# Reordering the first loads and casts of a two-layer hybrid decoder trunk

## The chip, the cores and the metric

The kernel runs on one core of one Trainium2 chip. The metric is the device time of one execution in microseconds (us). The kernel before took 1221.57 us, the median of 3 runs (1221.18 to 1221.61). The profiled execution, from which all the rows below come, took 1221.98 us.

## The reference, cut to what matters

The input `x` is 512 tokens by 1024 features, in float32. Two layers follow each other. Each has a token mixer and a gated ConvFFN, and each of the four sublayers ends in `LayerNorm(alpha * x + f(x))`. The mixer of layer 0 is gated linear attention (GLA), the mixer of layer 1 gated DeltaNet. Only the very beginning of GLA is touched by the change:

```python
def gla_mixer(x, w_in, w_gk2, b_gk, norm_w, w_out):
    hk, hv = GLA_HEADS * GLA_DK, GLA_HEADS * GLA_DV          # 512, 1024
    proj = x @ w_in                                          # w_in: 1024 x 3088
    q, k, v, gate, gk_lr = jnp.split(proj, [hk, 2 * hk, 2 * hk + hv, 2 * hk + 2 * hv], axis=-1)
    gk = jax.nn.log_sigmoid((gk_lr @ w_gk2 + b_gk).astype(jnp.float32)) / GLA_NORMALIZER
    ...
```

## The kernel before, in words

**Products.** Every float32 operand is split into two fp32r parts, `h` (a cast) and `l` (what the cast loses): `xh`, `xl` for x, `wh`, `wl` for a weight. A product is then three matmuls, `wh*xh + wh*xl + wl*xh`. The cast is normally made by ScalarE (ACT) and the subtraction by VectorE (DVE); `split_out` (L715) records both. TensorE (PE) is the engine with the most work.

**x.** x is loaded in eight tiles of 128 tokens by 512 features, called `h` (names h_99 and so on, 256 KB each). The two tiles that hold tokens 0 to 127 and 128 to 255 of features 0 to 511 are h_99 and h_101, here called the first quarters. The other halves of the same tokens are h_100 and h_102, and the later tokens are h_103 to h_106. `x_part` (L766) turns a tile with four PE transposes into a bank `xT` and splits it into `xh` and `xl`.

**Weights of the projection.** An item `fm` is a block of 128 columns of `w_in`, 1024 by 128, loaded into a buffer `raw` (512 KB; three such buffers). The first two items (raw_109 and raw_114) are loaded, cast and used in two halves of 256 KB. The third item is `rep`, a small one (64 KB), the fourth is raw_219, loaded whole. `open_items` (L522) multiplies the first two items with the first 256 tokens, half by half. The `rep` item and raw_219 follow, on the first 256 tokens and then on the rest.

**v's weights.** v and the gate are made by a scheme with seven products of quarter size. Some of its weight quarters, named `b11`, are kept in buffers `gw` (two of 512 KB) over several products, and loaded by `gated_load` (L438) as far ahead as the plan looks. The first products of this scheme come after all items of q and k.

**What sets the order.** The kernel is written in program order, and a scheduling layer places each instruction on its engine. `keep_in_program_order` pins an instruction. `behind(a, b)` (L703) says that `a` stands after `b` in the order, and adds no wait by itself. Each engine then runs its own instructions strictly in this order and waits on semaphores. DMA transfers are issued by SyncE (SP, most of them), by ACT (`nc.scalar.dma_start`) and by GpSimd (POOL). Transfers issued by SP go into one hardware queue (q1), those of ACT into another (q10), those of POOL into a software queue (q0). All of them run on the same 16 DMA engines.

**The opening.** `load_x` (L776) issues the two first quarters, then `prefetch`, which issues the first weights. It records a copy on ACT that loads an activation table, and three products `warm` of a column of ones, which need nothing but a memset. These keep PE busy from the start of the kernel on. Then come the cast of the first half weight (`split(0)`), the two `x_part`s, and `behind` calls that fix how ACT and DVE interleave these.

Of the kernel before, what the change touches and what calls it, by code (L numbers as in the profile page):

```python
# [17 lines left out]
S = 512  # L18
NTB = S // P
NC = D // P  # L20
# [14 lines left out]
GATED_NEW = {"b21": "b21", "b11": "b11", "t1": "b12", "b22": "b22"}  # L35
# [37 lines left out]
def blk(i, n=P):  # L73
    return slice(i * n, i * n + n)


class Trunk:
# [214 lines left out]
    def issue(self, item):  # L292

        nc = self.nc
        if item[0] == "rep":
            return self.issue_rep(*item[1:])
        if item[0] == "pad":
            return self.issue_pad(*item[1:])
        if item[0] == "fold":
            return self.issue_fold(*item[1:])  # L300
        if item[0] == "gated":
            return self.issue_gated(*item[1:])
        raw = self.rp.tile([P, 1024], F32, name=self.uid("raw"), tag="raw")
        used = 1024
        if item[0] == "fm":
            _, w, col = item
            r3 = raw.rearrange("p (c f) -> p c f", c=NC)
            w3 = w[:, col:col + P].rearrange("(c p) f -> p c f", p=P)
            part = lambda queue, c, n: queue.dma_start(r3[:, c:c + n, :], w3[:, c:c + n, :])
            if self.issued > 1:  # L310
                part(nc.sync, 0, NC)
            else:
                if self.issued == 0:
                    part(nc.scalar, 0, 4)
                    self.arriving(0, 1)
                else:
                    part(nc.sync, 0, 4)
                    self.arriving(1, 1)
                self.late.append(lambda: part(nc.sync, 4, 4))
                if self.issued:  # L320
                    for load in self.late:
                        load()
        else:
            _, w, row, n, col, _ = item
            used = n * S
            self.load = nc.sync.dma_start(
                raw[:, :used].rearrange("p (j f) -> p j f", j=n),
                w[row:row + n * P, col:col + S].rearrange("(j p) f -> p j f", p=P))
        if self.in_slots(item):
            w = []  # L330
            for j in range(used // S):
                wh, wl = self.room("wsh"), self.room("wsl")
                self.slotted = self.split_out(wh, wl, raw[:, blk(j, S)])
                self.vec(0.7)
                w.append((wh, wl))
            return w
        self.held += 1
        wh = self.wp.tile([P, 1024], F32R, name=self.uid("wh"), tag="wh")
        wl = self.wp.tile([P, 1024], F32R, name=self.uid("wl"), tag="wl")
        pieces = [blk(j, S) for j in range(used // S)] if self.issued < 2 else [slice(0, used)]  # L340
        split = lambda cols: self.split_out(wh[:, cols], wl[:, cols], raw[:, cols])
        if self.issued < 2:
            self.pieces += [lambda cols=cols: split(cols) for cols in pieces]
        elif self.issued < 4:
            self.opening(*split(pieces[0]))
        else:
            self.split = parts = split(pieces[0])
            for ins, other in zip(parts, self.after):
                if other is not None:
                    self.behind(ins, other)  # L350
        self.vec(1.24)
        return [(wh[:, blk(j, S)], wl[:, blk(j, S)]) for j in range(used // S)]
# [85 lines left out]
    def gated_load(self, group, name, i):  # L438


        if name not in GATED_NEW:
            return
        if name == "b11":
            t = self.mp.tile([P, 1024], F32, name=self.uid("gw"), tag="gw", bufs=2)
        else:
            t = self.rp.tile([P, 1024], F32, name=self.uid("raw"), tag="raw")
        self.nc.sync.dma_start(t.rearrange("p (j f) -> p j f", j=2), self.gated_rows(group, GATED_NEW[name], i))
        group[name, i] = t

    def issue_gated(self, group, name, i):  # L450
# [325 lines left out]
    def load_x(self, x):  # L776

        nc = self.nc
        self.h = [[self.resid("h") for _ in range(2)] for _ in range(NTB)]

        def load(tb, hf):
            nc.sync.dma_start(self.h[tb][hf], x[blk(tb), blk(hf, S)])
            self.set(("h", tb, hf))


        for tb in range(2):
            load(tb, 0)
        self.arriving = load
        self.look = 2
        self.prefetch()  # L790
        self.look = 0

        self.tc.keep_in_program_order(nc.scalar.copy(self.warm, self.one))
        ps = self.psum("warm")
        ones = self.one.to_broadcast([P, S])
        for n in (S, S, 64):
            self.tc.keep_in_program_order(
                nc.tensor.matmul(ps[:, :n], ones[:, :P], ones[:, :n], start=True, stop=True))
        split = lambda i: self.pieces[i]()
        piece = split(0)  # L800
        first = self.x_part(0, 0)
        second = self.x_part(1, 0)

        self.behind(first[0], piece[0])
        self.behind(second[0], first[0])
        self.behind(second[1], first[1])
        self.behind(piece[1], second[1])
        self.first = (second[0], piece[1])
        self.opening(*split(2))

        def arrive(i):
            self.opening(*self.x_part(i, 1))
            self.opening(*split(2 * i + 1))
            if i:
                self.look = 1
                self.prefetch()
                for tb in range(2, NTB):
                    for hf in range(2):
                        load(tb, hf)
                self.look = LOOKAHEAD  # L820
                self.prefetch()

        self.arrive = arrive
        for tb in range(2):
            self.set(("x", tb))

        def second():
            for tb in range(2, NTB):
                for hf in range(2):
                    self.last = self.x_part(tb, hf)  # L830
                yield 1.2

        self.spawn(second(), 7.0)
# [1235 lines left out]
```

## Time and profile before

| What | us |
|---|---|
| median of the runs | 1221.57 |
| the profiled execution's own time | 1221.98 |
| its span, from the first to the last instruction | 1220.2 |
| PE busy in it | 1213.6 |
| DVE busy | 906.1 |
| ACT busy | 609.4 |
| GpSimd busy | 160.7 |

The span is 1.78 us shorter than the execution's own time: this much lies around it. The profiled execution took 0.41 us longer than the median of the runs. All times in rows of the trace are microseconds from the start of the span. A row of the timeline gives start, duration, engine, line, operation, `output<-input`, shape and number of instructions, and in brackets the time for which the engine was idle before it and what ended that. `SPq` and `ACTq` are the issuing parts of these engines, `PEld` is PE's loading of weights, which overlaps its products. PE rows of products overlap each other, because products are pipelined: the time that one takes from the stream is the distance from its start to the next start. A row of the DMA issues ends with the time from the issue to the landing.

### The profile page before, as it was taken

The page shows a single profiled execution, that of the slowest core. Times are in us where ns is not written, and L with a number is a line of the kernel's source. Part 1 is how long each engine was busy: PE and PEld are TensorE (multiplying, and loading weights), DVE is VectorE, ACT ScalarE, POOL GpSimd, SP SyncE. Part 2 cuts the span into 40 slices and gives each one's busy share as a digit, 9 for nine tenths or more (in the row PEclk, how much of TensorE's full clock was granted, in tenths as well). Part 3 has the DMA queues.
Part 4 walks back from the last instruction along what each step waited for, and adds up shares of the span by engine and source line. Part 5 has one row for each costly group of instructions (what it writes and reads, how often), then busy time and mean ns, then how long its engine had stood idle before and what let it go on. Part 6 is the DMA issues. An engine that isn't in the chain of part 4 may idle for free.

```text
span 1220.2 us, 17190 instructions
## 1 busy us (share of the span) xinstructions
PE 1213.6 (99%) x6501; PEld 1025.1 (84%) x6501; DVE 906.1 (74%) x1515; ACT 609.4 (50%) x1072; POOL 160.7 (13%) x203
## 2 busy tenths in 40 slices
PE   9999999999999999999999999999999999999998
PEld 8888888988888888889888888988988888888886
DVE  6989787787757675666789965688687757776667
ACT  5666663544434443454678555544644433443440
POOL 3030101601100110001242030200510100020000
PEclk9999999999999999999999999999999999999999
DMA  8384642536743554433444351335444853383311
GB/s 227 113 164 115 141 154 72 189 105 137 190 122 92 124 95 121 123 102 91 125 125 130 87 136 36 101 107 156 135 125 101 170 178 95 104 171 97 108 65 69
DMA packets 176275, 149.41 MB, mean 122 GB/s; under 512 B 16870, under 2 KB 140842, under 8 KB 176192
## 3 DMA queue, kind: packets, MB, share of 16 engines
q1 hardware_dynamic: 162464, 116.28, 32.2%
q0 software_dynamic: 12768, 31.37, 13.0%
q8 instruction: 51, 0.84, 0.3%
q10 hardware_dynamic: 960, 0.66, 0.2%
q14 instruction: 32, 0.26, 0.1%
HBM read 129.92 MB, written 5.78 MB: 111 GB/s over the span
## 4 chain that ended last, share of the span: by engine, by line
PE 97%; DMA 1%; ACT 1%; DVE 1%; SPq 0%; issue 0%; DVEq 0%
PE fm L213 54%; PE fold L213 19%; PE tm L213 15%; PE o L213 2%; PE xT L231 1%; DMA raw<-in_gla_w_in_dram 1%; PE pq L213 1%; PE pg L213 1%; PE vn L213 1%; PE yT L231 1%; PE V L213 0%; PE ds L213 0%; PE qs L213 0%; PE s L213 0%; PE ks L213 0%; DMA raw<-in_gdn_w_in_dram 0%
## 5 line engine op out<-in xcount | busy, mean ns | idle before, releaser
L213 PE MATMUL fm<-xh,wh 128*128 128x512 f32 (+2 forms) x1096 | 400.4, 368 | 0.7 <-ACT xh L716 0.7
L213 PE MATMUL fm<-xl,wh 128*128 128x512 f32 (+2 forms) x1096 | 398.5, 366 | 0.0
L213 PE MATMUL fm<-xh,wl 128*128 128x512 f32 (+1 forms) x1072 | 391.5, 367 | 0.2 <-DVE wl L716 0.2
L716 DVE TENSOR_TENSOR wl<-raw,wh 128x1024 fp32r<-128x1024 f32 (+1 forms) x158 | 195.4, 1239 | 151.7 <-ACT wh L716 151.3
L716 ACT CAST wh<-raw 128x1024 fp32r<-128x1024 f32 (+1 forms) x159 | 164.9, 1039 | 211.2 <-PE fm L213 135.5
L213 PEld LDWEIGHTS fm<-xh,wh 128*128 128x128 f32 (+1 forms) x1096 | 205.4, 188 | 34.1 <-ACT xh L716 0.9
L213 PEld LDWEIGHTS fm<-xl,wh 128*128 128x128 f32 (+1 forms) x1096 | 205.4, 188 | 32.6
L213 PEld LDWEIGHTS fm<-xh,wl 128*128 128x128 f32 x1072 | 201.2, 189 | 33.7 <-DVE wl L716 0.4
L1019 DVE SCALAR_TENSOR_TENSOR conv<-fm,ffn_cw,conv 128x511 f32<-128x511 f32 x112 | 83.5, 745 | 9.6 <-ACT conv L1017 7.9
L213 PE MATMUL fold<-wh,fh 128*128 128x512 f32 x224 | 87.6, 391 | 0.0
L213 PE MATMUL fold<-wh,fl 128*128 128x512 f32 x224 | 87.2, 389 | 0.0
L213 PE MATMUL fold<-wl,fh 128*128 128x512 f32 x224 | 87.1, 389 | 0.0
L716 ACT CAST wh<-b 128x1024 fp32r<-128x1024 f32 x48 | 50.0, 1054 | 74.2 <-PE fold L213 32.5
L716 DVE TENSOR_TENSOR wl<-b,wh 128x1024 fp32r<-128x1024 f32 x48 | 58.1, 1222 | 22.7 <-ACT wh L716 22.5
L412 POOL DMA_DIRECT2D b<-b x24 | 20.8, 902 | 357.2 <-DVE wl L716 306.7
L1037 ACT ACTIVATE conv<-conv 128x512 f32<-128x512 f32 x44 | 27.8, 632 | 63.3 <-DVE conv L1019 63.3
L1585 DVE SCALAR_TENSOR_TENSOR conv<-fm,gdn_cw,conv 128x511 f32<-128x511 f32 (+2 forms) x72 | 54.0, 788 | 5.1 <-ACT conv L1583 4.6
L213 PEld LDWEIGHTS fold<-wh,fh 128*128 128x128 f32 x224 | 42.0, 188 | 9.6 <-DVE h L1108 1.0
L213 PEld LDWEIGHTS fold<-wh,fl 128*128 128x128 f32 x224 | 42.0, 188 | 8.8
L213 PEld LDWEIGHTS fold<-wl,fh 128*128 128x128 f32 x224 | 42.1, 188 | 8.6
L1019 DVE SCALAR_TENSOR_TENSOR form<-fm,ffn_cw,form 128x511 f32<-128x511 f32 x64 | 47.7, 745 | 1.1
L929 POOL TENSOR_TENSOR h<-h,gb 128x512 f32<-128x512 f32 x16 | 24.1, 1525 | 135.5 <-PE xT L231 134.2
(363 smaller groups left out, 2009.1 us busy)
## 6 DMA issues: line engine op xcount, KB each, us to landing
raw<-in_ffn_w_in_dram SPq DMA_DIRECT2D x88, 512.0 KB, 3.9
raw<-in_gdn_w_in_dram SPq DMA_DIRECT2D x32, 512.0 KB, 4.1
b<-in_ffn_w_out_dram SPq DMA_DIRECT2D x24, 512.0 KB, 6.0
b<-b POOLq DMA_DIRECT2D x24, 512.0 KB, 4.8
raw<-in_ffn_w_out_dram SPq DMA_DIRECT2D x20, 512.0 KB, 3.7
raw<-in_gla_w_in_dram SPq DMA_DIRECT2D x18, 512.0 KB, 4.4
gw<-in_gla_w_in_dram POOLq DMA_DIRECT2D x8, 512.0 KB, 7.5
raw<-in_gla_w_out_dram SPq DMA_DIRECT2D x8, 512.0 KB, 3.7
```

Source lines behind the costliest of these rows:

```text
L213: t = self.nc.tensor.matmul(out, a, b, start=start, stop=stop, skip_group_check=joined)
L231: t = self.nc.tensor.transpose(out, a, self.ident[:n, :n])
L412: self.nc.gpsimd.dma_start(out, group[src, i][:, cols], accum_op=ALU.add)
L716: return self.nc.scalar.copy(dst_h, src), self.nc.vector.tensor_sub(dst_l, src, dst_h)
L929: nc.gpsimd.tensor_mul(h[hf], h[hf], gb[hf])
L1019: nc.vector.scalar_tensor_tensor(a[:, d:], ps[:, :S - d], tap(2 - d), a[:, d:], ALU.mult, ALU.add)
L1037: nc.scalar.activation(a, a, AF.Gelu)
L1585: self.conv = nc.vector.scalar_tensor_tensor(a[:, d:], ps[:, :S - d], tap(3 - d), a[:, d:], ALU.mult, ALU.add)
```

## The change

There are four edits, all in the opening of the first layer.

- The first half of the first weight (raw_109) is issued by SP instead of ACT, behind both first quarters of x, which SP issues.
- That half is cast by VectorE (`tensor_copy`) instead of ScalarE. Its subtraction stays on VectorE.
- The second of the three `warm` products has 256 columns instead of 512.
- The loads of the kept weights `b11` of v (and of the gate) get a `behind` on the last load that an `fm` item or an output projection recorded in `self.load`.

The calls in `load_x` are put in another order, and the `behind` calls change to suit.

```diff
@@ issue @@
             if self.issued > 1:
-                part(nc.sync, 0, NC)
+                self.load = part(nc.sync, 0, NC)
             else:
                 if self.issued == 0:
-                    part(nc.scalar, 0, 4)
+                    part(nc.sync, 0, 4)
                     self.arriving(0, 1)
...
         if self.issued < 2:
             self.pieces += [lambda cols=cols: split(cols) for cols in pieces]
+            if self.issued == 0:
+                self.pieces[0] = lambda cols=pieces[0]: (
+                    nc.vector.tensor_copy(wh[:, cols], raw[:, cols]),
+                    nc.vector.tensor_sub(wl[:, cols], raw[:, cols], wh[:, cols]))
@@ gated_load @@
-        self.nc.sync.dma_start(t.rearrange("p (j f) -> p j f", j=2), self.gated_rows(group, GATED_NEW[name], i))
+        load = self.nc.sync.dma_start(t.rearrange("p (j f) -> p j f", j=2),
+                                      self.gated_rows(group, GATED_NEW[name], i))
+        if name == "b11":
+            self.behind(load, self.load)
         group[name, i] = t
@@ load_x @@
-        for n in (S, S, 64):
+        for n in (S, 256, 64):
             self.tc.keep_in_program_order(
                 nc.tensor.matmul(ps[:, :n], ones[:, :P], ones[:, :n], start=True, stop=True))
         split = lambda i: self.pieces[i]()
-        piece = split(0)
         first = self.x_part(0, 0)
         second = self.x_part(1, 0)
-
-        self.behind(first[0], piece[0])
+        piece = split(0)
+
         self.behind(second[0], first[0])
+        self.behind(first[1], piece[0])
         self.behind(second[1], first[1])
         self.behind(piece[1], second[1])
```

What this does to the order is seen on two engines. On SP, at the start of the program, the queue held before (h are the tiles of x, raw the weights):

```order
L782 DMA h_99<-in_x_dram 128x512
L782 DMA h_101<-in_x_dram 128x512
L782 DMA h_100<-in_x_dram 128x512
L309 DMA raw_114<-in_gla_w_in_dram 128x4x128
L782 DMA h_102<-in_x_dram 128x512
L309 DMA raw_109<-in_gla_w_in_dram 128x4x128
```

and holds now:

```order
L789 DMA h_99<-in_x_dram 128x512
L789 DMA h_101<-in_x_dram 128x512
L309 DMA raw_109<-in_gla_w_in_dram 128x4x128
L789 DMA h_100<-in_x_dram 128x512
L309 DMA raw_114<-in_gla_w_in_dram 128x4x128
L789 DMA h_102<-in_x_dram 128x512
L309 DMA raw_109<-in_gla_w_in_dram 128x4x128
```

The first half of raw_109, which ACT issued before, has come into SP's queue as the third transfer; everything behind it is one place later.

On SP again, further down, where raw_219 and the later items of q and k are loaded, with the rows taken out:

```order
 L309 DMA raw_219<-in_gla_w_in_dram 128x8x128
-L447 DMA gw_661<-in_gla_w_in_dram 128x2x512
-L447 DMA gw_709<-in_gla_w_in_dram 128x2x512
 L309 DMA raw_379<-in_gla_w_in_dram 128x8x128
 L309 DMA raw_419<-in_gla_w_in_dram 128x8x128
```

and where they stand now:

```order
L309 DMA raw_480<-in_gla_w_in_dram 128x8x128
L309 DMA raw_539<-in_gla_w_in_dram 128x8x128
L309 DMA raw_603<-in_gla_w_in_dram 128x8x128
L451 DMA gw_661<-in_gla_w_in_dram 128x2x512
L451 DMA gw_709<-in_gla_w_in_dram 128x2x512
L451 DMA raw_609<-in_gla_w_in_dram 128x2x512
```

The two loads of v's kept weights have moved back past five loads of q's and k's weights. The later pair of such loads, for the gate, keeps its place in SP's order.

On PE, at the start of the program, one piece of the difference:

```order
-L798 MATMUL warm_122<-one_87 128x512 x2
-L798 MATMUL warm_122<-one_87 128x64
-L231 MATMUL xT_128<-ident_86,h_99 128x128 x4
-L231 MATMUL xT_135<-ident_86,h_101 128x128 x4
+L805 MATMUL warm_122<-one_87 128x512
+L805 MATMUL warm_122<-one_87 128x256
+L805 MATMUL warm_122<-one_87 128x64
+L231 MATMUL xT_126<-ident_86,h_99 128x128 x4
+L231 MATMUL xT_133<-ident_86,h_101 128x128 x4
 L213 MATMUL fm_174<-xh,wh_112 128x256 x4
```

Apart from the shorter product (and new numbers in names) PE's order is the same to the end of the program. ACT loses one DMA issue and one cast, DVE gets that cast as its first work behind two memsets, ahead of `xl<-xT`; POOL's order is unchanged.

## The prediction

> **What bounds the kernel now.** I read the page first, for the engine that sets the end:
>
> ```profile
> PE 1213.6 (99%) x6501; PEld 1025.1 (84%) x6501; DVE 906.1 (74%) x1515; ACT 609.4 (50%) x1072; POOL 160.7 (13%) x203
> PE 97%; DMA 1%; ACT 1%; DVE 1%; SPq 0%; issue 0%; DVEq 0%
> ```
>
> PE is busy for 1213.6 of the 1220.2 us, and 97% of the chain that ended last is PE. An edit that touches only the opening can gain no more than PE loses there. So I read the chain of waits in order of time, from its start:
>
> ```profile
> 0.81 3.62 DMA raw<-in_gla_w_in_dram
> 4.45 0.66 SPq L358
> 5.14 2.77 SPq L782
> 9.38 6.33 DMA raw<-in_gla_w_in_dram
> 15.73 1.06 ACT wh L716
> 16.82 1.24 DVE wl L716
> 18.10 8.65 PE fm L213 x70
> ```
>
> This is the row that decides. Up to 18.10 us the chain doesn't run over PE at all: it runs over loads. The load issued at 9.38 is raw_219, the fourth item of q and k. It lands at 15.71, its cast and its subtraction follow, and PE goes on at 18.10. From there on the chain is PE's. The timeline of PE around that point:
>
> ```profile
> 17.48 0.28 PE L213 MATMUL fm<-xh,wh 128*128 128x256 f32 x1
> 17.60 0.28 PE L213 MATMUL fm<-xl,wh 128*128 128x256 f32 x1
> 18.10 0.39 PE L213 MATMUL fm<-xh,wl 128*128 128x256 f32 x1 [0.22 <-DVE wl L716]
> ```
>
> These are the first products of raw_219. From start to start one takes 0.12 us (17.48 to 17.60), and the next needs `wl` and starts 0.50 later: PE loses 0.38 us. Whatever PE gains ahead of this place, it waits that much longer here, unless raw_219 lands earlier. When it lands is asked of the stretches of the trace (the last two columns are the DMA engines' busy share and GB/s; shares over 1 come of overlapping packets):
>
> ```profile
> 2.00:3.00 1.00, 1.00 (x3) 0.48 (x2) 0.00 (x0) 0.80 (x2) 1.00 (x2) 1.00 0.78 228
> 3.00:4.00 1.00, 1.00 (x3) 0.48 (x2) 0.00 (x0) 0.00 (x0) 1.00 (x3) 1.00 1.12 328
> 4.00:5.00 1.00, 1.00 (x4) 0.48 (x4) 0.00 (x0) 0.55 (x1) 1.00 (x3) 1.00 0.86 290
> 9.50:11.50 2.00, 2.00 (x20) 2.00 (x19) 1.52 (x4) 1.51 (x4) 0.00 (x0) 1.00 0.96 314
> 13.50:15.50 2.00, 2.00 (x20) 2.00 (x19) 0.00 (x0) 0.00 (x0) 1.90 (x4) 1.00 1.10 371
> ```
>
> The DMA engines are full from 3 us on, before raw_219 and while it comes in. So its landing is set by the bytes ahead of it, and not by when it is issued.
>
> **The change part by part.** First the start of PE's work, by the timeline of the opening:
>
> ```profile
> 0.99 4.10 PE L798 MATMUL warm<-one 128*128 128x512 f32 x6 [0.99 <-POOL one L102]
> 2.00 0.34 PEld L798 LDWEIGHTS warm<-one 128*128 128x128 f32 x1 [0.52 <-issue]
> 2.85 0.34 PEld L798 LDWEIGHTS warm<-one 128*128 128x128 f32 x1 [0.52 <-issue]
> 4.45 0.62 ACT L716 CAST wh<-raw 128x512 fp32r<-128x512 f32 x1 [1.65 <-DMA raw<-in_gla_w_in_dram]
> 4.88 1.57 PE L231 MATMUL xT<-ident,h 128*128 128x128 f32 x8
> 5.98 1.09 ACT L716 CAST xh<-xT 128x512 fp32r<-128x512 f32 x2 [0.91 <-PE xT L231]
> 7.12 0.74 PE L213 MATMUL fm<-xh,wh 128*128 128x256 f32 x4 [0.68 <-ACT xh L716]
> 14.79 1.03 PE L231 MATMUL xT<-ident,h 128*128 128x128 f32 x8
> ```
>
> *The shorter product.* A product of 512 columns runs as two passes, and the weight loads at 2.00 and 2.85 show 0.85 for one pass. Half the columns out of two passes is 0.85 us. The first transpose then starts at 4.88 - 0.85 = 4.03, if its data are there:
>
> ```profile
> h<-in_x_dram SPq DMA_DIRECT2D x1, 256.0 KB, 2.8
> 1.25 0.42 SPq L782 DMA_DIRECT2D h<-in_x_dram  x1
> h<-in_x_dram SPq DMA_DIRECT2D x1, 256.0 KB, 4.2
> q10 hardware_dynamic: 236, 0.12, 114.3%
> ```
>
> The first row is h_99, issued at 0.81: it lands at 3.6, in time. The next two are h_101: issued at 1.25, it lands at 5.4.
>
> *The weight moved behind both tiles of x.* The last row is ACT's queue between 3.25 and 3.60: raw_109's half, issued by ACT at 0.81 and landed at 4.43 (the chain's first row), took all 16 engines there. Taken out from ahead of h_101, its 256 KB at 290 to 328 GB/s are worth 0.80 to 0.90 us: h_101 lands at about 4.5, ahead of the 4.88 at which PE can now use it. The weight lands about 0.9 later, at 5.3. On SP every later transfer is issued 0.42 later (the row at 1.25), which the full engines cover.
>
> *The transposes.* Eight took 1.57 us here and 1.03 us at 14.79. A slow one takes 0.85 / 4 = 0.21 and a fast one some 0.11, so about five of the eight were slow: PE's clock rose close to 6.0 us, 5.0 after PE's first work. Taken with the clock rising at that same time, all eight run slow now, from 4.03 to 5.73. The last is done with its pipeline at 5.94 (before, four slow ones started at 4.88 and ACT took their result 1.10 later, at 5.98; now the second four start at 4.88). The cast of 0.59 follows at 5.98, and the first `fm` product at 6.62, instead of 7.12: 0.50 us earlier. Were the clock to rise with the work and not with the time, this would be 0.85; were it not to rise at all, see the third rival.
>
> *The cast on VectorE.* The row nearest to it is the same cast, of other data:
>
> ```profile
> L909 DVE CAST xh<-xf 128x512 fp32r<-128x512 f32 x12 | 5.3, 443 | 9.3 <-ACT xf L905 9.3
> 7.47 0.62 ACT L716 CAST wh<-raw 128x512 fp32r<-128x512 f32 x1 [0.40 <-DMA raw<-in_gla_w_in_dram]
> 9.12 0.65 PE L213 MATMUL fm<-xh,wh 128*128 128x256 f32 x4
> ```
>
> 0.44 us, from 5.3 to 5.8, ahead of the 6.6 at which PE wants it: nothing on the path, with 0.8 to spare. Behind it on VectorE stand the subtractions for `xl`, which need ACT's casts at 5.7 and 6.6 anyway. ACT loses 0.62 of work from 4.45 on, while it had nothing else; that cast held nobody. The issue of a DMA that ACT loses stood ahead of its table load, far from the path.
>
> *What follows up to 17.48.* The lead of 0.50 must survive the other loads. The next is the half of raw_114, cast by ACT until 8.09 and used by PE at 9.12, now at 8.62: 0.5 to spare, with a landing that has the same bytes ahead of it as before. I take the lead as kept in whole, with zero as the other bound, since it makes no difference: PE comes to `wl` of raw_219 with 0.38 + 0.50 = 0.88 us in hand. Up to 0.88 may be lost in the opening and the end stays.
>
> *raw_219 itself.* Ahead of it are the same eight tiles of x, both split weights and `rep`; raw_109's half is now in SP's queue instead of ACT's, on the same engines. At the start one queue could feed less than two: 328 GB/s with two (3 to 4 us) against 290 with one (4 to 5 us) is 38 KB in that us, or 0.1 us. The loads of `gw` stood behind raw_219 in the same queue and delay nothing ahead of them. So the landing moves by 0 to +0.1, and I take 0. Bounds: it can't be worth more than the whole 0.88 to the good; to the bad it is the 0.42 by which each issue on SP is later, if the engines run dry once.
>
> *v's kept weights.* Rows of SP, ACT and the stretches behind the opening:
>
> ```profile
> 9.86 1.41 SPq L447 DMA_DIRECT2D gw<-in_gla_w_in_dram  x2
> 28.02 2.84 SPq L309 DMA_DIRECT2D raw<-in_gla_w_in_dram  x2
> 35.48 0.37 SPq L447 DMA_DIRECT2D raw<-in_gla_w_in_dram  x1
> 44.09 1.05 ACT L716 CAST wh<-raw 128x1024 fp32r<-128x1024 f32 x1
> 55.00 1.03 ACT L716 CAST wh<-gw 128x1024 fp32r<-128x1024 f32 x1
> raw<-in_gla_w_in_dram SPq DMA_DIRECT2D x1, 512.0 KB, 4.2
> 25.00:35.00 10.00, 10.00 (x71) 9.26 (x70) 9.94 (x16) 8.45 (x11) 0.00 (x0) 1.00 0.39 107
> ```
>
> Now they are issued behind raw_603 (the second issue in the row at 28.02, over at 30.86), and use 1 MB: at 314 GB/s 3.3 us. With the 4.2 us that raw_603 takes to land, they are there by about 39, 16 us before the first cast of `gw` at 55.00. Behind them SP issues raw_609 (35.48), which may land some 2 us later, near 41, against its cast at 44.09: covered. raw_379 and the next lose 1 MB ahead of them and land up to 3.3 us earlier, for nobody: PE is busy for the whole of 25 to 35 us, and no wait of it ends on a load there.
>
> **Sum.** Opening -0.50, waited for again at raw_219 +0.50, landing 0, casts 0, `gw` 0: the profiled execution stays at 1221.98, and the median of the runs, 0.41 below it, at 1221.57. I forecast 1221.6.
>
> **The rivals.** *First, raw_219 lands earlier.* While it came in, the engines moved 371 GB/s, part of it for the `gw` loads behind it; if those took engine time from its last packets, it lands earlier without them. For it: the transfers overlap in time. Against it: they share one queue, and the next weights take `gw`'s place there. The whole of 0.88 gives 1220.7; half of it 1221.1.
>
> *Second, slower: one queue at the start runs dry.* In SP's queue the weight is issued only at about 1.7, and all behind it 0.42 later. If the engines are idle for that long once before 9 us, raw_219 and with it 18.10 move by 0.42: 1222.0. For it: 228 GB/s in the third us. Against it: the engines' share of 0.86 and more afterwards, and issues of 0.42 against 0.85 for the transfer of a tile. It decides once raw_219 lands after 15.8.
>
> *Third, PE's clock rises later.* PE pauses now from 5.94 to 6.62, and the products ahead are shorter. If the 5.0 us of slow work were counted anew from 6.62, PE would work at half speed for 5.0 us and lose 2.5; less the 0.88 in hand that is +1.6, 1223.2. Against it: before, PE paused as long (0.68 in the row at 7.12) and ran fast behind it. [...]
>
> **How the numbers follow.** Forecast (within 0.3 of 1221.6) 0.62; first rival 0.16; second 0.15; third 0.07. The range of 8 in 10 takes in the first rival in full and the second with the runs' own spread (0.4): 1220.6 to 1222.4. A measurement of this kernel tells 0.2%, 2.4 us, from no change. No gain reaches this: all of PE's waits in the opening are 0.88. The third rival at its worst is at +1.6. So same 0.95; faster 0.02 and slower 0.03 for what is not in the sum.
>
> **What would show it.** In the profile after: the first transpose near 4.0 instead of 4.88 and the first `fm` product near 6.6; VectorE's cast of 0.44 us after the weight's landing near 5.3; raw_219 landing within 0.3 of 15.7; a wait of PE for `wl` there of 0.7 to 0.9 us instead of 0.38; PE's steady work from 18.1; `gw` issued near 31 and no new wait of PE up to 60. The forecast is wrong if raw_219 lands well away from 15.7, or if PE's transposes and first products are still slow behind 7 us.

## The result and the profile after

The changed kernel takes 1223.49 us, the median of 21 runs (1221.91 to 1224.71). The kernel before takes 1221.34 (21 runs, 1220.90 to 1221.87). The ratio is 1.0017, with a 95% interval of 1.0011 to 1.0023: 2.15 us slower. The difference is smaller than the 0.2% that was called no change, but the time lies 1.1 us above the predicted range. The profiled execution of the changed kernel took 1223.49, the median itself.

The page has nothing new to say on the bound (first the span, then PE's row, then the shares of the chain):

```profile
span 1221.8 us, 17190 instructions
PE 1214.0 (99%) x6501; PEld 1026.5 (84%) x6501; DVE 909.4 (74%) x1516; ACT 609.8 (50%) x1071; POOL 162.3 (13%) x203
PE 99%; DMA 0%; DVE 0%; SPq 0%; ACT 0%; issue 0%; DVEq 0%
```

The span grew by 1.6 us, PE's busy time by only 0.4. The rest is idle time of PE. The busy time itself says little here: the shorter product takes 0.85 us out of it, and products that run at half the clock, seen below, put time in. The timeline of the opening shows where the loss lies:

```profile
0.99 3.25 PE L805 MATMUL warm<-one 128*128 128x512 f32 x6 [0.99 <-POOL one L102]
4.03 1.47 PE L231 MATMUL xT<-ident,h 128*128 128x128 f32 x8
7.66 0.71 PE L213 MATMUL fm<-xh,wh 128*128 128x256 f32 x4 [2.16 <-ACT wh L723]
9.80 1.05 PE L213 MATMUL fm<-xh,wl 128*128 128x256 f32 x4
10.65 1.05 PE L213 MATMUL fm<-xh,wh 128*128 128x256 f32 x4
13.01 0.64 PE L213 MATMUL fm<-xh,wh 128*128 128x256 f32 x4
19.75 0.28 PE L213 MATMUL fm<-xh,wl 128*128 128x256 f32 x1
5.53 1.99 DVE L346 CAST wh<-raw 128x512 fp32r<-128x512 f32 x1 [3.92 <-DMA raw<-in_gla_w_in_dram]
5.29 1.94 POOL L1352 MEMSET sc<- 128x512 f32 x4
```

The opening goes as predicted up to the transposes at 4.03. Then the cast, moved to VectorE, takes 1.99 us, and PE stands idle for 2.16. The first `fm` product starts at 7.66, where it was to start at 6.62. From there things get worse, not better: the product at 13.01 is the one that before started at

```profile
10.98 0.64 PE L213 MATMUL fm<-xh,wh 128*128 128x256 f32 x4
```

So a loss of 0.54 us at the first product (7.66 against 7.12) has become 2.03 here (13.01 against 10.98). In between, a group of four takes 0.85 us from one start to the next (the group at 9.80 is followed by one at 10.65), where before it took 0.48. The stretches of the trace give the reason; the number ahead of the DMA share is the granted clock:

```profile
4.91:8.32 3.41, 1.25 (x11) 1.04 (x10) 2.79 (x3) 1.69 (x3) 2.32 (x5) 1.00 1.11 339
8.32:11.73 3.41, 3.41 (x19) 3.40 (x18) 2.78 (x5) 1.10 (x2) 0.00 (x0) 0.50 1.12 300
11.73:14.00 2.27, 2.27 (x21) 2.27 (x21) 1.12 (x2) 1.52 (x3) 0.37 (x1) 1.00 1.12 330
```

PE was busy for 1.25 of the 3.41 us up to 8.32. Then its clock was halved for 3.41 us, while it had work all the time.

That this is the usual case, and not one odd execution, can be read from the mean granted clock, which is on record for every run. Fifteen of the 21 runs have 0.998 or 0.999, and all of them took 1223.16 to 1223.78. Six have 1.000: three at 1221.91 to 1222.17, one at 1223.05, and the two slowest, 1224.49 and 1224.71. (A value of 0.999 alone proves little, since in the profile of the changed kernel the clock also falls at the very end of the span, to 0.76 from 1219 to 1221 and 0.50 behind that: 22 of the 87 runs of the kernel before, beside the experiments, have it too. None of them has 0.998.)

The last step is the place that bounded the kernel before. The product that needs raw_219's `wl` starts at 19.75 instead of 18.10, 1.65 later, which is the growth of the span. There is no bracket on this row: `wl` was there long before, and the wait of 0.38 has gone. In the chain of waits (start, duration, what), PE follows without a break once the opening is over, and the loads that stood there before are no longer in it:

```profile
2.73 4.27 DMA raw<-in_gla_w_in_dram
7.03 0.63 ACT wh L723
7.66 0.71 PE fm L213 x4
```

One name here misleads. The chain and the bracket of the row at 7.66 name ACT's cast of raw_114's half, which ended at 7.66. The first products don't need that half; they need raw_109's, cast by VectorE until 7.52. A wait is put down to what came last by the profile, and the two casts ended within 0.14 us of each other. The experiments below show which one it was.

### The profile page after: what moved, and what is told of

Same layout as the page of the kernel before. It is cut to its first block, busy times and chain, and to the rows that moved or that the text cites. A ratio compares the mean times of both kernels' runs of the same rounds, so it can differ in the third digit from the quotient of the medians.

```text
span 1221.8 us, 17190 instructions
## 1 busy us (share of the span) xinstructions
PE 1214.0 (99%) x6501; PEld 1026.5 (84%) x6501; DVE 909.4 (74%) x1516; ACT 609.8 (50%) x1071; POOL 162.3 (13%) x203
## 4 chain that ended last, share of the span: by engine, by line
PE 99%; DMA 0%; DVE 0%; SPq 0%; ACT 0%; issue 0%; DVEq 0%
PE fm L213 55%; PE fold L213 19%; PE tm L213 16%; PE o L213 2%; PE xT L231 1%; PE pq L213 1%; PE vn L213 1%; PE pg L213 1%; PE yT L231 1%; PE V L213 0%; PE ds L213 0%; PE s L213 0%; PE qs L213 0%; PE ks L213 0%; DMA raw<-in_gla_w_in_dram 0%; PE sa L213 0%
```

## The experiments

Three explanations had to be told apart. One: GpSimd's memsets hold the cast, and the pause that follows halves PE's clock. Two: the loads are later because one queue issues them all at the start. Three: the lead that the shorter product gives is lost in some other way. All experiments ran beside the kernel before, whose median was 1221.25 (27 runs), 1221.31 (33) and 1221.31 (27) in the three sets. Where a kernel adds work, the result of that work isn't used.

### The memsets out of the cast's way

GpSimd clears four `sc` tiles just when the cast runs. Here they are recorded behind the loads of `gk` on GpSimd and run from 15.6 us on. (All else as in the changed kernel.)

```diff
             for i in range(6):
-                nc.gpsimd.dma_start(raw[16 * i:16 * i + 16, :], w_gk2)
+                self.gk_load = nc.gpsimd.dma_start(raw[16 * i:16 * i + 16, :], w_gk2)
+            self.set(("gk",))
...
             t = self.slot("sc")
-            nc.gpsimd.memset(t, 0.0)
             sct.append(t)
+        def zero():
+            yield from self.until(("gk",))
+            for t in sct:
+                self.behind(nc.gpsimd.memset(t, 0.0), self.gk_load)
+        self.spawn(zero())
```

> The changed kernel with one more edit: GpSimd's four memsets (sc, 128x512 each) stand behind its six gk loads instead of ahead of them, so that they run well after 12 us. Theory A (the cast on VectorE is held up by GpSimd's memsets, which ran from 5.29 to 7.23): the cast takes 0.44 us and ends at 5.97, PE's first fm product starts at 6.2 (then ACT's second cast for xh sets it) instead of 7.66, the clock doesn't drop, and PE's steady work begins right behind wl of raw_219, near 17.6 (before 18.10, changed kernel 19.75): 1220.8 us, 0.5 below the kernel before. Theory B (the cast is slow there by itself, on data just landed and with all DMA engines busy): the cast still takes 2.0 us, first fm product at 7.66, 1223.5 us.

Measured: 1221.98 (11 runs, 1221.09 to 1222.41), ratio to before 1.0004 [0.9996, 1.0013]. The timeline of this kernel:

```profile
6.45 0.43 DVE L346 CAST wh<-raw 128x512 fp32r<-128x512 f32 x1 [4.84 <-DMA raw<-in_gla_w_in_dram]
7.02 0.71 PE L213 MATMUL fm<-xh,wh 128*128 128x256 f32 x4 [1.19 <-DVE wh L346]
18.27 0.38 PE L213 MATMUL fm<-xh,wl 128*128 128x256 f32 x1 [0.20 <-DVE wl L723]
```

The same cast now takes 0.43 us, as it was predicted, and the clock doesn't fall: behind a pause of 1.19 us it is 1.00 in every stretch up to 20 us. The first product follows its end (6.88) by 0.14, as it did in the changed kernel (7.52 and 7.66): so the cast on VectorE was what PE had waited for. Of the 2.15 us, 1.5 come back; the expected 1220.8 is not reached. What stays is at the other end of the opening: the weight landed only at 6.43, raw_219 at 15.88, and PE waits for `wl` again.

### The cast back on ACT

As the changed kernel, with the cast on ScalarE behind both casts of `xh`; the memsets stay.

```diff
-            if self.issued == 0:
-                self.pieces[0] = lambda cols=pieces[0]: (
-                    nc.vector.tensor_copy(wh[:, cols], raw[:, cols]),
-                    nc.vector.tensor_sub(wl[:, cols], raw[:, cols], wh[:, cols]))
...
-        self.behind(first[1], piece[0])
+        self.behind(piece[0], second[0])
```

> The changed kernel with the cast of the first half weight back on ScalarE, behind both casts for xh; all else as changed (loads, shorter product, gw later, memsets where they were). Theory A and B alike: the cast takes 0.62 us on ACT and ends near 6.7, PE's first fm product starts near 6.75, no drop of the clock, steady work near 17.6: 1220.8 us. If instead the lateness came of the weight's later landing or of the shorter product, and not of the cast, the time stays near 1223.5.

Measured: 1222.42 (11 runs, 1220.93 to 1223.39), ratio 1.0008 [0.9999, 1.0017]. In the timeline:

```profile
6.47 0.62 ACT L719 CAST wh<-raw 128x512 fp32r<-128x512 f32 x1
7.14 0.74 PE L213 MATMUL fm<-xh,wh 128*128 128x256 f32 x4 [1.19 <-ACT wh L719]
```

Beside the same memsets, ACT's cast takes the 0.62 that it took before. Of the two casts it is VectorE's that they hold. The first product starts at 7.14, as before the change (7.12): with the cast behind the late landing of the weight, near 6.3, the shorter product brings nothing. At the other end raw_219 lands at 15.92 and PE waits for its `wl`, as in the experiment before; here too the expected 1220.8 is missed. The runs spread over 2.5 us, so that this median is a rough one.

### Each memset done twice

The dose: as the changed kernel, with every memset repeated.

```diff
             nc.gpsimd.memset(t, 0.0)
+            nc.gpsimd.memset(t, 0.0)
```

> The changed kernel with each of GpSimd's four memsets done twice, so that they last 1.9 us longer (to about 9.1). Theory A: the cast on VectorE ends 1.9 us later, near 9.4, the first fm product near 9.5; with PE's clock as slow as before behind that, about 1225.4 us. Theory B: the cast ends at 7.5 as before, the time stays near 1223.5.

Measured: 1225.72 (4 runs, 1224.95 to 1226.34), ratio 1.0036 [1.0022, 1.0050]. Rows of the timeline, the first and the last pair of memsets, and stretches with the granted clock:

```profile
5.28 1.00 POOL L1352 MEMSET sc<- 128x512 f32 x2
8.08 1.01 POOL L1353 MEMSET sc<- 128x512 f32 x2
5.33 4.05 DVE L346 CAST wh<-raw 128x512 fp32r<-128x512 f32 x1 [3.72 <-DMA raw<-in_gla_w_in_dram]
9.52 1.20 PE L213 MATMUL fm<-xh,wh 128*128 128x256 f32 x4 [3.94 <-DVE wh L346]
...
8.50:11.90 3.40, 2.38 (x11) 2.41 (x12) 3.26 (x5) 0.29 (x1) 0.59 (x2) 0.50 1.07 293
11.90:15.20 3.30, 3.30 (x17) 3.30 (x17) 1.29 (x2) 0.99 (x3) 0.00 (x0) 0.50 0.81 232
```

With twice the memsets, GpSimd is done at 9.09 instead of 7.23 and the cast at 9.38 instead of 7.52: it ends some 0.3 us behind the last memset in both. It doesn't run slower beside them; it waits for the whole run of them. Here PE's pause is longer, 3.94 us against 2.16, and the clock stays halved for twice as long, from 8.5 to 15.3.

### The cast on VectorE alone

The kernel before, with only the cast moved to VectorE. The weight stays in ACT's queue, the memsets stay where they are.

```diff
+            if self.issued == 0:
+                self.pieces[0] = lambda cols=pieces[0]: (
+                    nc.vector.tensor_copy(wh[:, cols], raw[:, cols]),
+                    nc.vector.tensor_sub(wl[:, cols], raw[:, cols], wh[:, cols]))
...
-        self.behind(first[0], piece[0])
+        self.behind(first[1], piece[0])
```

> The kernel before with one edit: the cast of the first half weight on VectorE instead of ScalarE. Its load is still the first on ACT's queue and lands at 4.43, ahead of GpSimd's memsets (5.28 to 7.22). Theory A: the cast takes 0.44 us (4.45 to 4.9), the first fm product stays at 7.12, no change of time, 1221.3 us. Theory B: the cast takes about 2.0 us here too, until 6.45, and the subtractions for xl behind it start late; the first fm product is still set by xh at 7.12, the time changes by less than 0.3 us, so the duration of the cast tells.

Measured: 1221.31 (11 runs, 1220.89 to 1221.76), ratio 1.0000 [0.9992, 1.0009]. The timeline:

```profile
4.79 0.82 DVE L346 CAST wh<-raw 128x512 fp32r<-128x512 f32 x1 [3.18 <-DMA raw<-in_gla_w_in_dram]
4.78 0.52 POOL L1577 DMA_DIRECT2D gdn_al<-in_gdn_dt_bias_dram  x1
5.28 2.18 POOL L1349 MEMSET sc<- 128x512 f32 x4
6.77 0.74 PE L213 MATMUL fm<-xh,wh 128*128 128x256 f32 x4 [0.67 <-ACT xh L720]
17.35 0.34 PE L213 MATMUL fm<-xh,wl 128*128 128x256 f32 x1
```

The cast costs nothing here. Issued by ACT, the weight lands at 4.77, ahead of the memsets. The cast takes 0.82 instead of 0.43. GpSimd was issuing a DMA until 5.30, and the cast ended 0.3 behind that; but that this issue held it is not shown, for in the kernel with the weight back in ACT's queue, below, the cast starts at 4.83, within the same issue (4.77 to 5.35), and takes 0.43. In turn the four memsets take 2.18 instead of 1.94; the first of them started at 5.28, while the cast still ran. So the new cast is not bad by itself. It became bad because another of the edits had its data land between 5.3 and 7.2.

### PE kept busy through the pause

As the changed kernel, with three more products of ones (512 columns each) on PE between the second tile's transposes and the first `fm` product. The memsets still hold the cast.

```diff
         second = self.x_part(1, 0)
+        for _ in range(3):
+            self.tc.keep_in_program_order(
+                nc.tensor.matmul(ps[:, :S], ones[:, :P], ones, start=True, stop=True))
         piece = split(0)
```

> The changed kernel with three more products of ones (512 columns each) on PE between the second tile's transposes and the first fm product, so that PE isn't idle there; the cast on VectorE is as late as in the changed kernel (7.5). Theory C (of the 1.65 us that PE's steady work is later, the pause of 2.2 us costs 1.5 by the slow clock that follows it, from 8.3 to 11.7): the first fm product still starts at 7.66, the clock stays fast, and PE's steady work begins near 18.2: 1221.4 us, 2.1 below the changed kernel. Theory D (the clock is slow for its own reasons, or the late start alone costs the time): 1223.5 us or more.

Measured: 1222.54 (11 runs, 1221.82 to 1223.26), ratio 1.0010 [1.0001, 1.0019]. Rows of the timeline and one stretch:

```profile
6.14 1.37 DVE L346 CAST wh<-raw 128x512 fp32r<-128x512 f32 x1 [4.54 <-DMA raw<-in_gla_w_in_dram]
5.29 2.75 PE L811 MATMUL warm<-one 128*128 128x512 f32 x6
7.65 0.87 PE L213 MATMUL fm<-xh,wh 128*128 128x256 f32 x4
18.54 0.28 PE L213 MATMUL fm<-xh,wl 128*128 128x256 f32 x1
...
8.50:11.50 3.00, 3.00 (x27) 2.90 (x25) 2.60 (x5) 1.56 (x3) 0.00 (x0) 1.00 1.10 282
```

This separates the late start from the clock. The cast ends at 7.51 and the first product starts at 7.65, as in the changed kernel. But the clock stays at 1.00 where it had been 0.50, and the product of raw_219's `wl` comes at 18.54 instead of 19.75. The halved clock was thus a large part of the loss: 1.2 us at this product (0.8 in the whole span), and 0.95 in the medians. What is left is 1.2 us over the kernel before, where 0.1 was expected. Most of it is the late start: the kernel with ACT's queue and 512 columns, below, starts its first product at 6.82 and the product of `wl`, for which it doesn't wait, at 17.38, so that this one is 0.83 and then 1.16 behind.

From the start of this product of `wl` to the end of the span, all thirteen profiles of this document take 1201.7 to 1202.4 us, whatever the kernel. So everything that the variants win or lose is decided ahead of it, and a single span tells nothing below some 0.7 us.

### The same without the memsets

The first experiment with two such products.

```diff
         second = self.x_part(1, 0)
+        for _ in range(2):
+            self.tc.keep_in_program_order(
+                nc.tensor.matmul(ps[:, :S], ones[:, :P], ones, start=True, stop=True))
```

> The first experiment (GpSimd's memsets late) with two products of ones as filler ahead of the first fm product. Its runs lay in two groups, near 1221.2 and near 1222.3. [...] Theory E (the upper group are executions in which the first weight or raw_219 landed late, from one queue at the start): both groups stay, median near 1222.

Measured: 1222.10 (11 runs, 1221.48 to 1223.19), ratio 1.0008 [0.9999, 1.0017]. Against the first experiment (1221.98) this is nothing: with the memsets gone, a pause of 1.19 us is left to fill, and raw_219, landed at 16.00, sets the end in any case. So something beside memsets and clock holds this kernel 0.8 us above the kernel before.

### The weight back in ACT's queue

The first experiment, with raw_109's half issued by ACT again.

```diff
                 if self.issued == 0:
-                    part(nc.sync, 0, 4)
+                    part(nc.scalar, 0, 4)
```

> The first experiment (memsets late) with the first half weight issued by ACT's own queue again. The weight then lands at 4.4 and the second tile of x at 5.4, as before the change; the first fm product near 6.7. Theory E: what is left of the loss (0.7 us) goes, 1221.2 us, and raw_219 lands no later than 15.7. Theory C: the pause of PE shortens from 1.2 to about 0.9 us or is split by the wait for the second tile, so part of the upper group goes too; the traces tell the two apart by the landings and by the distance of PE's products.

Measured: 1221.56 (11 runs, 1220.90 to 1224.46), ratio 1.0008 [0.9999, 1.0017]. This median hides two groups. Seven runs lie between 1220.90 and 1221.64, as the kernel before; four lie at 1222.95, 1222.97, 1224.16 and 1224.46. The profiled execution is of the first group (1220.90). In its timeline:

```profile
5.49 0.66 PE L231 MATMUL xT<-ident,h 128*128 128x128 f32 x4 [0.43 <-DMA h<-in_x_dram]
6.83 0.74 PE L213 MATMUL fm<-xh,wh 128*128 128x256 f32 x4 [0.67 <-ACT xh L723]
```

With the weight in ACT's queue, h_101 lands later, and PE, early by the shorter product, waits 0.43 us for it. The two pauses of PE now follow each other closely. The next two experiments ask whether the second group is theirs.

### The shorter product alone, and the longer one again

The kernel before with one number changed:

```diff
-        for n in (S, S, 64):
+        for n in (S, 256, 64):
```

> The kernel before with one edit: the second product of ones has 256 columns instead of 512. Theory C (pauses of PE in the opening let its clock stay or fall to half for a while, in some executions): PE waits for the second tile of x (5.4) and for ACT's casts, its work before 7 us is shorter by 0.85, and some of the eleven runs lie 1.5 to 3 us above the others, as 4 of 11 did in the seventh experiment; the rest near 1221.3. If the short product costs nothing by itself, all runs lie between 1220.7 and 1222.0.

Measured: 1221.75 (11 runs, 1220.91 to 1224.27), ratio 1.0007 [0.9998, 1.0016]. Again two groups: six runs at 1220.91 to 1221.75, and 1222.76, 1222.78, 1222.85, 1224.10 and 1224.27. This time the profiled execution (1222.76) is of the second group. Rows of its timeline, and its stretches:

```profile
5.66 0.66 PE L231 MATMUL xT<-ident,h 128*128 128x128 f32 x4 [1.02 <-DMA h<-in_x_dram]
6.99 0.86 PE L213 MATMUL fm<-xh,wh 128*128 128x256 f32 x4 [0.68 <-ACT xh L716]
...
4.00:7.40 3.40, 1.71 (x13) 1.23 (x13) 1.13 (x2) 1.71 (x4) 3.22 (x7) 1.00 0.97 314
7.50:10.80 3.30, 3.30 (x17) 3.30 (x17) 2.65 (x5) 1.60 (x3) 0.00 (x0) 0.50 1.20 290
```

Two pauses of 1.02 and 0.68 us leave PE busy for 1.71 of 3.40 us, and the clock is halved from 7.4 to 10.8. No cast of VectorE is in it. The shorter product makes the fall possible by itself: PE runs out of work sooner, ahead of loads that come no earlier. It is shown for this one execution only. Of the other four runs of the upper group, each has a mean granted clock of 1.000; the four of the experiment before have 0.999, against 1.000 in its other seven.

The other way round, the weight in ACT's queue and the memsets late, with 512 columns:

```diff
-        for n in (S, 256, 64):
+        for n in (S, S, 64):
```

> The same as the tenth with the first weight's half issued by ACT's queue again; what is left of the change is the cast on VectorE and the later gw loads. Theories C and E: 1221.3 us, no difference from the kernel before, all runs between 1220.7 and 1222.0; raw_219 lands between 14.8 and 15.7.

Measured: 1221.22 (11 runs, 1220.90 to 1221.83), ratio 1.0000 [0.9991, 1.0009]: one group. With the longer product and the weight in ACT's queue (this kernel, the one with the cast alone, and the one with `gw` alone below), none of 33 runs is above 1221.83. With the shorter one and the weight in ACT's queue, 9 of 22 are at 1222.76 or more.

### One queue alone

The last kernel with the weight in SP's queue: memsets late, 512 columns, and so of the change only the queue, the cast and `gw`.

```diff
                 if self.issued == 0:
-                    part(nc.scalar, 0, 4)
+                    part(nc.sync, 0, 4)
```

> The changed kernel with two edits undone or taken out of the way: GpSimd's memsets late, and the second product of ones back at 512 columns. What is left of the change that can cost is the one queue at the start (the weight on SP behind both tiles of x). Theory C: no run with a slow clock, so the spread is below 1.5 us. Theory E: raw_219 lands 0.4 to 0.6 later than with ACT's queue, PE waits for it, and the median stays 0.4 to 0.7 above the kernel before: 1221.8. Without theory E: 1221.3.

Measured: 1222.02 (11 runs, 1221.46 to 1222.77), ratio 1.0005 [0.9996, 1.0014], 0.8 above the kernel with ACT's queue, on the same chip. The intervals of the two ratios overlap, but eight of its eleven runs lie above all eleven of the other kernel. The landings show where it comes from. First this kernel (the stretch in which the queues differ most, SP's issue of raw_219 and the loads behind it, ACT's cast of raw_219, which starts 0.02 behind its landing, and the product of its `wl`), then the same with ACT's queue:

```profile
3.50:4.00 0.50, 0.50 (x2) 0.29 (x1) 0.00 (x0) 0.00 (x0) 0.50 (x2) 1.00 0.82 208
9.84 8.82 SPq L309 DMA_DIRECT2D raw<-in_gla_w_in_dram  x4
15.96 1.05 ACT L723 CAST wh<-raw 128x1024 fp32r<-128x1024 f32 x1 [4.31 <-DMA raw<-in_gla_w_in_dram]
18.32 0.38 PE L213 MATMUL fm<-xh,wl 128*128 128x256 f32 x1 [0.53 <-DVE wl L723]
```

```profile
3.50:4.00 0.50, 0.50 (x2) 0.29 (x1) 0.00 (x0) 0.00 (x0) 0.50 (x2) 1.00 1.20 356
9.19 8.53 SPq L309 DMA_DIRECT2D raw<-in_gla_w_in_dram  x4
15.01 1.05 ACT L723 CAST wh<-raw 128x1024 fp32r<-128x1024 f32 x1 [3.60 <-DMA raw<-in_gla_w_in_dram]
17.38 0.38 PE L213 MATMUL fm<-xh,wl 128*128 128x256 f32 x1
```

With one queue the engines moved 208 GB/s at a time when with two queues they moved 356. In the same half us it was 171 to 224 in all seven profiles of kernels in which SP issues the weight, and 332 to 370 in the six in which ACT does. This half us is not the loss, though. From 2 to 5 us taken together the seven moved 264 to 289 GB/s and the six 272 to 286, which is the same. What stays different is when SP comes to issue raw_219: 9.84 here, 9.19 with ACT's queue. In all thirteen profiles it lands 5.6 to 6.3 us behind its issue. The issue comes at 9.04 to 9.38 in the six and in the changed kernel, and at 9.62 to 10.11 in the other six kernels with SP's queue; four of these, from 9.84 on, moved 250 to 278 GB/s between 9 and 12 us, where all the others moved 304 to 339. Why SP gets there later was not found.

Here raw_219 lands at 15.94 instead of 14.99, and PE starts its `wl` product 0.94 later. Over all profiles, raw_219 landed between 15.15 and 16.00 (mean 15.66, seven kernels) where SP issues the weight, and between 14.81 and 15.71 (mean 15.11, six kernels, the one before among them) where ACT does. The two ranges overlap, and the mean difference is 0.5.

### `gw` alone

The kernel before with only the loads of the kept weights moved.

```diff
-                part(nc.sync, 0, NC)
+                self.load = part(nc.sync, 0, NC)
...
-        self.nc.sync.dma_start(t.rearrange("p (j f) -> p j f", j=2), self.gated_rows(group, GATED_NEW[name], i))
+        load = self.nc.sync.dma_start(t.rearrange("p (j f) -> p j f", j=2),
+                                      self.gated_rows(group, GATED_NEW[name], i))
+        if name == "b11":
+            self.behind(load, self.load)
```

> The kernel before with one edit: v's kept weights loaded behind raw_603, as in the change. If the loads of gw behind raw_219 take nothing from it: raw_219 lands at 14.9 to 15.7, as in two traces of the old order, no change, 1221.3 us. If they do: it lands 0.5 earlier, and the time falls by up to 0.4, to 1220.9 (PE comes to its wl at 17.6 and can't gain more).

Measured: 1221.39 (11 runs, 1220.70 to 1221.70), ratio 0.9999 [0.9991, 1.0008]. raw_219 in the profile:

```profile
15.23 1.05 ACT L719 CAST wh<-raw 128x1024 fp32r<-128x1024 f32 x1 [3.87 <-DMA raw<-in_gla_w_in_dram]
17.59 0.39 PE L213 MATMUL fm<-xh,wl 128*128 128x256 f32 x1
```

It landed at 15.21, 0.5 ahead of the profile of the kernel before (15.71). That looks like a gain until it is held against the others: with the old place of `gw` the cast-only kernel had 14.92, with the new one the two kernels with ACT's queue had 14.81 and 14.99. The landing varies by that much from one profile to the next, and the times show no gain.

## Why the prediction was wrong

**The step that failed** is "The cast on VectorE": "0.44 us, from 5.3 to 5.8 ... nothing on the path, with 0.8 to spare". The landing was right (5.50), the cost of the cast alone too (0.43 without the memsets). What was left out is what else ran at that time. The profile before showed it in one row, which stood there to be read:

```profile
5.28 1.94 POOL L1345 MEMSET sc<- 128x512 f32 x4
```

It also gave a sign that the two engines hold each other. Here is a subtraction on VectorE that takes 0.68 to 0.69 in 18 of its 24 instances, beside an operation of GpSimd:

```profile
204.28 1.52 DVE L913 TENSOR_TENSOR xl<-xf,xh 128x512 fp32r<-128x512 f32 x1
203.96 1.30 POOL L929 TENSOR_TENSOR h<-h,gb 128x512 f32<-128x512 f32 x1 [2.32 <-PE xT L231]
```

The mean of the casts, 443 ns, hid this: one of those twelve took 0.67. Beside the memsets the cast waited not for one of 0.54 us but for all four in a row, 1.99 against 0.43, and 4.05 with eight.

**Price of the failed step.** Taken with that, the sum would have had the cast end near 7.5 and the first product start at 7.65, 0.5 late instead of 0.5 early. The prediction's own reserve ("up to 0.88 may be lost in the opening and the end stays") would have covered part of it. It did not cover what followed.

**The third rival, PE's clock**, was right in kind and had a chance of 0.07. It was expected as a rise that comes late. In the trace it is a fall after a rise: transposes that start 0.21 us apart up to 4.88 and some 0.12 apart behind it, a pause of 2.16 us, and the half clock from 8.32 to 11.73. It costs 1.49 us (2.03 less 0.54), where half of 3.41 us would be 1.71. The 1223.2 that the rival gave is close to the 1223.49 measured, though for a reason that was not in it: the pause came from the cast, which the forecast had as covered. The argument against it, that PE had paused for 0.68 us before and ran fast behind that, held for one pause of that size and not for one of 2.16. The forecast also took the rise itself, near 6.0, from one execution. The trace's record of the full clock begins at 5.95 in the kernel before and at 4.90 in the changed kernel, and in the kernel with the cast alone the products of ones took 3.58 us instead of 4.10. So there was no fixed 5.0 us to reckon with.

**The second rival, one queue that runs dry**, holds in its size, at +0.5 (the mean landings) to +0.9 us (the last two kernels) instead of 0.42. Its mechanism is shown in part only. The engines do move less from 3.5 to 4.0, 171 to 224 GB/s against 332 to 370, and by 5 us they have made it up. What is later is SP's issue of raw_219, by 0.65 in the last two kernels, and the landing followed the issue in every profile. The prediction had set this aside ("set by the bytes ahead of it, and not by when it is issued"). Whether the bytes ahead hold the issue up in turn is open. In the changed kernel this price doesn't add to the others, since PE now comes to raw_219's `wl` later than the load does. It shows once the memsets are out of the way, as the 0.7 us that then remain. But it has a second effect that counts: the weight lands at 5.3 to 6.4 instead of 4.4 to 4.8, which is what carries the cast into the memsets.

**The shorter product** was costed at 0.50 us to the good, and PE did start its transposes at 4.03, 0.85 earlier. This brought nothing anywhere: in the kernels without the memsets the first `fm` product came at 7.02 (weight in SP's queue) and 6.83 (in ACT's), against 6.73 and 6.82 with the longer product. Loads and the casts behind them set that time, not PE. What the edit did is to open pauses, 1.02 and 0.68 us in the kernel with it alone, and behind these the clock fell.

**The reserve at raw_219** was read from one execution. The 0.38 us wait for `wl` stands in the profile of the kernel before, where raw_219 landed at 15.71. In the other five kernels with ACT's queue it landed at 14.8 to 15.2, and PE waited there for 0.25 us or not at all (the product of `wl` after `gw` alone starts 0.37 behind the one ahead of it, of which 0.12 is its usual distance). That the profiled execution was 0.41 us above the median was noted and not used. Its wait is then hardly there in a typical run, and there a loss in the opening goes to the end almost in full. This is an inference from five profiles of other kernels: the kernel before has only the one. The sizes fit it. The 2.03 us lost by 13.01, without any reserve, come close to the 2.15 between the medians; between the two profiles, the reserve of 0.38 leaves 1.65.

**Right were** the transposes' start, the landing of the weight (5.50 for 5.3) and of h_101 (4.3 for 4.5), and all on `gw`: issued at 31.19 behind raw_603, with no wait of PE between 18 and 62 us, worth nothing either way (0.9999). The first rival was rightly set aside: the moved loads bring raw_219 in no earlier than the landings vary anyway.

**The sum as measured.** The cast alone 0, `gw` alone 0, the shorter product alone +0.4 in the median with a second group of runs up to 3 us slower, one queue some +0.7. No part costs 2 us. The cost is in their meeting: the queue delays the weight, the delay puts the cast beside the memsets, the shorter product empties PE's stream, and behind the pause of 2.16 us the clock is halved.

**Open** stays what decides between the two groups of runs. A fall of the clock is shown for the profile at 1222.76; the runs near 1224.2 were not profiled, nor the changed kernel's own at 1224.49 and 1224.71. These two have a mean granted clock of 1.000, so a fall like the profiled one didn't slow them. A rise that comes late, as the third rival had it, would not be seen in this number: the profile gives 1.00 ahead of the first rise too, while the changed kernel's transposes start 0.21 us apart there. No trace shows one. Nor was it found why the weight in SP's queue lands at 5.3 in one profile and at 6.4 in another. None of the variants beats the kernel before beyond its interval.

## What to carry to other kernels

Before an operation is moved to another engine, list what its neighbours do at that very time, and cost it with and without them: the cast on VectorE took 1.99 us beside four of GpSimd's memsets and 0.43 without. A pause of PE near the start can have two prices, the pause and the clock behind it: here the pause of 2.16 us made the first product 0.54 late, and the half clock cost 1.49 more. Behind a pause of 1.19, in the profile with the memsets late, the clock didn't fall. So look twice at an edit that lets PE run out of work sooner, ahead of loads that stay where they are: here it won nothing and opened the pauses. And a wait of a few tenths seen in one profile is no reserve: ask how much the landing behind it moves from one execution to the next.

## What the runs showed of the hardware

- **VectorE's cast waited for GpSimd's memsets, the whole row of them.** It took 0.43 us alone, 1.99 beside four memsets, 4.05 beside eight; it ended 0.3 us behind the last one each time. With the cast still running as the first memset started, the four took 2.18 instead of 1.94. Beside a DMA that GpSimd was issuing, the cast took 0.82 once and 0.43 once. The profile shows the wait as a long cast, not as idle time.
- **PE's clock was halved for 3.4 us, or for twice that.** It was 0.50 from 8.32 to 11.73 (3.41 us), in the kernel with the shorter product alone from 7.4 to 10.8, and with the longer pause from 8.5 to 15.3. In the 3.41 us ahead of the first of these falls PE was busy for 1.25, and in the 3.40 ahead of the second for 1.71. In the profile with the memsets late the clock stayed at 1.00 behind a pause of 1.19 us. In the kernel with each memset twice PE was busy for 2.38 of the 3.40 us from 8.50 on, and the clock stayed at 0.50 behind that; it was busy for all of 11.90 to 15.20, and the clock was 1.00 from 15.3 on.
- **The load that joined the queue of the others landed later, and so did raw_219 in the mean.** raw_109's half landed at 5.3 to 6.4 from SP's queue (seven profiles) and at 4.4 to 4.8 from ACT's (six); raw_219 landed 0.5 later in the mean. The rate of the 16 engines was lower with the one queue for half a us only (171 to 224 against 332 to 370 GB/s from 3.5 to 4.0). From 2 to 5 us it was the same (264 to 289 against 272 to 286).
